# Feed-forward parts of a two-layer decoder trunk: product slabs spread over all tiles, two tiles per vector operation, whole weight rows split

## The chip, the cores and the metric

One NeuronCore of a Trainium2 chip runs the whole program in one launch. The metric is device time in microseconds (us); a lower number is better. Five engines matter here: TensorE (PE, with its weight loads shown apart as PEld), VectorE (DVE), ScalarE (ACT), GpSimd (POOL) and SyncE (SP), whose queue issues the DMAs.

## The reference

Two decoder layers over 256 tokens of width 2048, all in float32. What matters here is the feed-forward part that ends each layer (inner width 8192):

```python
def squared_relu_mlp(h, w1, w2):
    z = jax.nn.relu(h @ w1)
    return (z * z) @ w2

# in each layer i, after the mixer and the memory cross-attention
x = x + jnp.concatenate([token_out, mem_out], axis=-1) @ w_out[i]
x = x + squared_relu_mlp(rms_norm(x, ffn_norm[i]), w_ff1[i], w_ff2[i])
```

Around it stand a pooling mixer (layer 0), shared keys and values computed from the stream after layer 0, differential attention (layer 1) and a memory cross-attention in both layers.

## The kernel before

**Numbers in two parts.** Every float32 operand is split into a high part, rounded to the format that TensorE multiplies (`fp32r`), and a low part, the rest. A product then takes high x high, high x low and low x high. The activations are kept as `x[:, k, 0:256]` (high) and `x[:, k, 256:512]` (low) for each chunk k of 128 features. The weights are split while the kernel runs: `Feed._split` (L142) lets ScalarE copy a chunk of raw weights into `hi_ring` (L147, a cast) and VectorE subtract that from the raw chunk into `lo_ring` (L148).

**The feed.** All weights lie in device memory in the order of use, as rows of eight 128x128 blocks (128x1024, 512 KB). `Feed.load` (L116) issues one DMA for each on SyncE (L129), three ahead. A *job* is a piece of split weights. An ordinary job `("N", n)` is half a row, four blocks, and takes one slot of 512 columns in each ring; there are six slots. A slot is used again when the job in it has been multiplied. `Feed.fill` (L180) prepares up to three jobs ahead. A first run of the program without instructions (`dry`) records the order.

**A tile.** A narrow tile makes 128 output features for 256 tokens: 16 blocks, each with a matmul of 512 columns (high weights times both parts) and one of 256 columns (low weights times the high part). `a_part` (L361) alternates the two; `a_pairs` (L372) issues the two 512-column matmuls of a pair of blocks and then the two of 256. The framework assigns the instructions to fixed queues for each engine ahead of time, by readiness and priority; within one engine the order is then fixed.

**The feed-forward part**, `ffn(l, xs, tags, done)` (L636). There are 64 up tiles (`up_tile`) and, for output features 0 to 1023, four rounds q of eight down tiles (`down_tile`). Layer 0 uses the alternating order (L364 and L365 for up, L722 and L723 for down), layer 1 the paired one (L381, L383). Each up tile is copied out of PSUM by ScalarE (`evict`, L658), its two halves are added (L702), relu and scale follow (L284), ScalarE squares (L706), and high and low parts go to `z` (L662, L665). Each of these is issued for one tile. Output features 1024 to 2047 use a product scheme of the Strassen-Winograd kind with seven products where eight would be needed: a *slab* is the pair of activation chunks 2i and 2i+1 with a 2x2 arrangement of weight blocks 512 columns wide. It needs four sums of the activations (`combine`, `sums_high`, `sums_low`, kept in `sit`) and four of the weights. The weight sums are made by VectorE in the raw tiles: a step `K` (L166, L167) and one at L175. A slab has four jobs: 0 (two chunks), 1 (one), 2 (two), 3 (two); they give 6, 3, 6 and 6 matmuls of 512 columns (L748 to L750). Their results add up in seven PSUM banks (tiles `p`) over all 32 slabs of a layer.

**The order.** Sixteen up tiles run with three PSUM banks (`ff`). Then `open_banks` takes the seven product banks, and only one bank is left for tiles, `x_bank`. Rounds q = 0, 1, 2 run 24 tiles each, with a slab spread over every three: in the gap before the first tile job 0, before the second jobs 1 and 2, before the third job 3. The eight slabs of the last quarter and the last eight down tiles are left to `last` (L841): two slabs each ahead of tiles 0, 1 and 2, one each ahead of 3 and 4. `finish_banks` (L788) then combines the seven banks, and TensorE transposes the result (tile `ct`, L813). Work behind a tile is put off by `at(d, fn)`, which runs `fn` after d ticks; a narrow tile has four ticks.

Raw rows have four buffers and the raw tiles of slabs three, so that the second load of a slab waits until job 3 of the slab before has been split.

Of the kernel before, what the change touches and what calls it, by code (L numbers as in the profile page):

```python
# [18 lines left out]
P = 128  # L19
T = 256  # L20
# [5 lines left out]
NBLK = 5796  # L26
SLOTS, AHEAD, LOADS, KOFF, RAWS = 6, 3, 3, 2, 4
CN = 0.5 ** (1.0 / 3.0)
# [27 lines left out]
class Plan:  # L56
# [7 lines left out]
    def __init__(self):  # L64
        self.entries = []
        self.npos = 0
        self.jobs = []
        self.slabs = []

    def close(self):  # L70
# [9 lines left out]
        for p in prep:  # L80
            if p[0] == "K":
                self.loads += [("S", p[1], 0), ("S", p[1], 1)]
            elif p[0] == "N" and p[1] % 2 == 0:
                self.loads.append(("N", p[1] // 2))
            self.need[p] = len(self.loads) - 1
# [12 lines left out]
class Feed:  # L98


    def __init__(self, nc, wst, wpool, rows, plan, dry):
# [7 lines left out]
        self.t1 = None  # L109
        if not dry:  # L110
            self.hi = wpool.tile([P, SLOTS * 512], F32R, name="hi_ring")
            self.lo = wpool.tile([P, SLOTS * 512], F32R, name="lo_ring")
            self.busy = [False] * SLOTS
# [19 lines left out]
    def _slots(self, n):  # L133
        a = self.at if self.at + n <= SLOTS else 0
# [4 lines left out]
        self.at = (a + n) % SLOTS  # L139
        return a  # L140

    def _split(self, job, src, n):  # L142
# [3 lines left out]
        hi, lo = self.hi[:, a * 512 : (a + n) * 512], self.lo[:, a * 512 : (a + n) * 512]  # L146
# [5 lines left out]
    def _prepare(self, p):  # L152
        sub, add = self.nc.vector.tensor_sub, self.nc.vector.tensor_add
        self.load(self.plan.need[p] + 1 + LOADS)
        if p[0] == "N":
# [8 lines left out]
        t1 = self.t1[p[1] % 2]  # L164
        if p[0] == "K":
            add(t1, ra[:, 0:512], rb[:, 0:512])  # L166
            sub(rb[:, 0:512], t1, rb[:, 512:1024])  # L167
# [23 lines left out]

    def quad(self, what):

        job = ("N", self.pos // 4)
        if self.dry:
            self.plan.entries.append(what)
            if self.pos % 4 == 0:
                self.plan.jobs.append(job)
            return Nothing(), Nothing()
        if self.pos % 4 == 0:  # L200
# [9 lines left out]
    def used(self, n=1):  # L210
        self.pos += n
        if self.dry:
            self.plan.npos = self.pos
        elif self.pos % 4 == 0:
# [17 lines left out]
    def job_used(self, n, j):  # L232
        if not self.dry:
            self.free(("S", n, j))

# [11 lines left out]
def program(ctx, tc, plan, dry, xT, memT, par, lam, cst, wst, yT):  # L247
# [152 lines left out]
    def wide_step(ps, what, xs, k):  # L400
        hi, lo = feed.quad(what)
        for t in range(2):
            xh = xs[:, k, t * P : t * P + P]
            xl = xs[:, k, T + t * P : T + t * P + P]
            nc.tensor.matmul(ps[t], xl, hi, start=k == 0, stop=False)  # L405
            nc.tensor.matmul(ps[t], xh, hi, start=False, stop=False)  # L406
            nc.tensor.matmul(ps[t], xh, lo, start=False, stop=k == NK - 1)  # L407
# [3 lines left out]
    def b_tile(ps, w, l, c, xs):  # L411
        for k in range(NK):
            wide_step(ps, (w, l, k, c, 4), xs, k)
# [222 lines left out]
    def ffn(l, xs, tags, done):  # L636

        z = sp.tile([P, NK, 512], F32R, tag=tags[0], name=f"z{l}")
        sit = sp.tile([P, 8, 1024], F32R, tag=tags[1], name=f"sit{l}")
        room = sp.tile([P, 6144], F32, tag="big", name=f"room{l}")
        stage = [room[:, T * j : T * j + T] for j in range(8)]
        sums = [room[:, 2048 + 512 * j : 2560 + 512 * j] for j in range(2)]
        feed.t1 = [room[:, 3072 + 512 * j : 3584 + 512 * j] for j in range(2)]
        outs = [room[:, 4096 + 512 * j : 4608 + 512 * j] for j in range(3)]  # L650
        r = []
        banks = []
        cnt = [0]

        def evict(ps):
            x = outs[cnt[0] % 3]
            cnt[0] += 1
            nc.scalar.copy(x, ps)  # L658
            return x

        def high(j):
            nc.scalar.copy(z[:, j, 0:T], stage[j % 8])  # L662

        def low(j):
            nc.vector.tensor_sub(z[:, j, T : 2 * T], stage[j % 8], z[:, j, 0:T].bitcast(F32))  # L665

        def combine(i):

            a11, a21 = stage[2 * i % 8][:, 0:P], stage[2 * i % 8][:, P:T]
            a12, a22 = stage[(2 * i + 1) % 8][:, 0:P], stage[(2 * i + 1) % 8][:, P:T]  # L670
            s1, s2, s3, s4 = (sums[i % 2][:, c * P : c * P + P] for c in range(4))
            nc.vector.tensor_add(s1, a21, a22)
            nc.vector.tensor_sub(s3, a11, a21)
            nc.vector.tensor_sub(s2, s1, a11)
            nc.vector.tensor_sub(s4, a12, s2)

        def sums_high(i):
            nc.scalar.copy(sit[:, i, 0:512], sums[i % 2])

        def sums_low(i):  # L680
            nc.vector.tensor_sub(sit[:, i, 512:1024], sums[i % 2], sit[:, i, 0:512].bitcast(F32))

        def convert(j, d):
            at(d, lambda: high(j))
            at(d + 2, lambda: low(j))
            if j % 2:
                i = j // 2
                at(d + 3, lambda: combine(i))
                at(d + 5, lambda: sums_high(i))
                at(d + 7, lambda: sums_low(i))  # L690

        def up_tile(q, i, ps):
            if l == 1:
                a_pairs(ps, "w_ff1", l, q * NK + i, range(NK), xs)
            else:
                a_part(ps, "w_ff1", l, q * NK + i, range(NK), xs)
            if not r:
                r.append(rstd_from("x"))
            y = evict(ps)

            def first():
                nc.vector.tensor_add(y[:, 0:T], y[:, 0:T], y[:, T : 2 * T])  # L702
# [638 lines left out]
```

## Time and profile before

| | |
|---|---|
| runs (3) | median 2067.43 us, 2067.31 to 2068.43 |
| profiled execution, its span | 2069.3 us |
| TensorE busy | 2057.2 us, 99% |
| weight loads (overlap) | 1754.1 us, 85% |
| VectorE busy | 1727.0 us, 83% |
| ScalarE busy | 1352.3 us, 65% |
| moved by DMA | 390.77 MB, mean 189 GB/s |

The profile gives the profiled execution no other time than its span, from the first to the last instruction. In its rows, a start is counted from the start of the span; `L381` is a line of the kernel, `x_bank<-fx,hi_ring` the tile that is written and those that are read, with buffer numbers left out, and `[0.77 <-PE x_bank]` idle time before an instruction and what ended it. A matmul's length in the trace includes its way through the array, so consecutive ones overlap: start to start is what counts. A row such as `p<-hi_ring,sit` belongs to a slab's product.

### The profile page before, as it was taken

What the parts mean: (1) busy time and instruction counts of PE and PEld (TensorE: products, weight loads), DVE (VectorE), ACT (ScalarE), POOL (GpSimd) and SP (SyncE); (2) the same over time, 40 slices, a digit from 0 to 9 for tenths busy, and PEclk for the clock granted to TensorE, in tenths of its full rate; (3) what the DMA queues carried; (4) which work ended last, traced back from release to release, by engine and by line L of the source; (5) the groups of instructions that cost most, each with busy time, mean ns of one, the idle gap of its engine ahead of it and who ended that gap; (6) DMA issues with size and microseconds to landing.
All of it is one profiled execution on the core that took longest, in us unless ns stands there. A gap on an engine that the chain in (4) does not pass through costs nothing.

```text
span 2069.3 us, 32331 instructions
## 1 busy us (share of the span) xinstructions
PE 2057.2 (99%) x11086; PEld 1754.1 (85%) x11086; DVE 1727.0 (83%) x3231; ACT 1352.3 (65%) x2505; POOL 55.6 (3%) x67
## 2 busy tenths in 40 slices
PE   9999999999999999999999999999999999999998
PEld 7888888888888888878888888888888888888877
DVE  8788888889878878999766688888879978988897
ACT  7765566666666656668665687567666666766664
POOL 0001300000000000000000000310000000000000
PEclk9999999999999999999999999999999999999999
DMA  8555555555555555455565433555556555555554
GB/s 311 171 186 186 189 186 178 189 195 202 184 197 192 193 205 191 168 188 184 187 231 193 163 133 110 186 193 186 183 191 207 192 194 201 189 207 188 193 188 144
DMA packets 110471, 390.77 MB, mean 189 GB/s; under 512 B 12256, under 2 KB 14944, under 8 KB 110304
## 3 DMA queue, kind: packets, MB, share of 16 engines
q1 hardware_dynamic: 110160, 388.59, 55.7%
q8 instruction: 87, 1.43, 0.3%
q14 instruction: 80, 0.66, 0.1%
q10 hardware_dynamic: 144, 0.10, 0.0%
HBM read 386.54 MB, written 2.10 MB: 188 GB/s over the span
## 4 chain that ended last, share of the span: by engine, by line
PE 52%; ACT 1%; DVE 1%; DMA 0%; issue 0%; ACTq 0%; DVEq 0%
PE x_bank L381 14%; PE x_bank L383 7%; PE ff L381 3%; PE wo L364 3%; PE p L748 2%; PE p L750 2%; PE p L749 2%; PE ff L383 2%; PE wo L365 1%; PE k L405 1%; PE k L407 1%; PE v L405 1%; PE v L406 1%; PE k L406 1%; PE v L407 1%; PE q L405 1%
## 5 line engine op out<-in xcount | busy, mean ns | idle before, releaser
L147 ACT CAST hi_ring<-raw 128x512 fp32r<-128x512 f32 x1193 | 736.0, 621 | 525.9 <-PE x_bank L381 134.0
L148 DVE TENSOR_TENSOR lo_ring<-raw,hi_ring 128x512 fp32r<-128x512 f32 x1193 | 826.0, 700 | 222.6 <-ACT hi_ring L147 192.0
L148 DVE TENSOR_TENSOR lo_ring<-slab,hi_ring 128x1024 fp32r<-128x1024 f32 x192 | 234.5, 1222 | 47.3 <-ACT hi_ring L147 42.7
L364 PE MATMUL x_bank<-fx,hi_ring 128*128 128x512 f32 x768 | 271.7, 397 | 0.0
L147 ACT CAST hi_ring<-slab 128x1024 fp32r<-128x1024 f32 x192 | 200.8, 1047 | 69.1 <-PE p L749 27.2
L381 PE MATMUL x_bank<-fx,hi_ring 128*128 128x512 f32 x768 | 240.7, 395 | 0.0
L365 PE MATMUL x_bank<-fx,lo_ring 128*128 128x256 f32 x768 | 214.8, 280 | 0.0
L364 PE MATMUL wo<-cat,hi_ring 128*128 128x512 f32 x512 | 182.3, 401 | 0.0
L364 PEld LDWEIGHTS x_bank<-fx,hi_ring 128*128 128x128 f32 x768 | 144.1, 188 | 37.7 <-ACT room L658 0.5
L383 PEld LDWEIGHTS x_bank<-fx,lo_ring 128*128 128x128 f32 x768 | 144.3, 188 | 33.6
L722 PE MATMUL x_bank<-z,hi_ring 128*128 128x512 f32 x480 | 170.0, 396 | 1.4 <-ACT room L658 0.9
L381 PE MATMUL x_bank<-z,hi_ring 128*128 128x512 f32 x480 | 151.2, 395 | 0.4 <-ACT hi_ring L147 0.4
L383 PE MATMUL x_bank<-fx,lo_ring 128*128 128x256 f32 x768 | 150.9, 278 | 0.0
L365 PEld LDWEIGHTS x_bank<-fx,lo_ring 128*128 128x128 f32 x768 | 144.8, 189 | 0.7
L365 PE MATMUL wo<-cat,lo_ring 128*128 128x256 f32 x512 | 143.6, 281 | 0.0
L723 PE MATMUL x_bank<-z,lo_ring 128*128 128x256 f32 x480 | 134.3, 280 | 0.0
L381 PEld LDWEIGHTS x_bank<-fx,hi_ring 128*128 128x128 f32 x768 | 120.5, 189 | 3.7
L364 PEld LDWEIGHTS wo<-cat,hi_ring 128*128 128x128 f32 x512 | 96.1, 188 | 23.8 <-DVE cat L284 0.3
L722 PEld LDWEIGHTS x_bank<-z,hi_ring 128*128 128x128 f32 x480 | 90.1, 188 | 24.6 <-ACT room L658 1.5
L383 PEld LDWEIGHTS x_bank<-z,lo_ring 128*128 128x128 f32 x480 | 90.1, 188 | 21.8 <-DVE lo_ring L148 1.0
L748 PE MATMUL p<-hi_ring,sit 128*128 128x512 f32 x256 | 101.9, 398 | 1.7 <-ACT hi_ring L147 1.3
L749 PE MATMUL p<-hi_ring,sit 128*128 128x512 f32 x256 | 100.3, 392 | 0.0
(317 smaller groups left out, 4195.1 us busy)
## 6 DMA issues: line engine op xcount, KB each, us to landing
raw<-in_w SPq DMA_DIRECT2D x595, 512.0 KB, 3.5
slab<-in_w SPq DMA_DIRECT2D x128, 512.0 KB, 3.5
resid<-in_x SPq DMA_DIRECT2D x8, 256.0 KB, 5.5
memraw<-in_mem SPq DMA_DIRECT2D x4, 512.0 KB, 3.7
out_y<-resid SPq DMA_DIRECT2D x16, 128.0 KB, 1.9
memraw<-in_mem SPq DMA_DIRECT2D x7, 256.0 KB, 6.8
raw<-in_w SPq DMA_DIRECT2D x3, 256.0 KB, 3.3
memraw<-in_mem SPq DMA_DIRECT2D x2, 128.0 KB, 4.4
```

The lines of the kernel that those rows point to most:

```text
L147: self.nc.scalar.copy(hi, src)
L148: self.nc.vector.tensor_sub(lo, src, hi.bitcast(F32))
L364: nc.tensor.matmul(ps, hi, xs[:, k, :], start=first and i == 0, stop=False)
L365: nc.tensor.matmul(ps[:, T : 2 * T], lo, xs[:, k, 0:T], start=False, stop=last and i == len(ks) - 1)
L381: nc.tensor.matmul(ps, hi, xs[:, k % NK, :], start=k == ks[0], stop=False)
L383: nc.tensor.matmul(ps[:, T : 2 * T], lo, xs[:, k % NK, 0:T], start=False, stop=k == ks[-1])
L405: nc.tensor.matmul(ps[t], xl, hi, start=k == 0, stop=False)
L406: nc.tensor.matmul(ps[t], xh, hi, start=False, stop=False)
L722: nc.tensor.matmul(ps, hi, z[:, i, :], start=a, stop=False)
L723: nc.tensor.matmul(ps[:, T : 2 * T], lo, z[:, i, 0:T], start=False, stop=b)
L748: nc.tensor.matmul(ps, a[1], hi, start=first, stop=False)
L749: nc.tensor.matmul(ps, a[0], hi, start=False, stop=False)
```

## The change

The feed-forward part is rewritten. The matmuls stay the same in number and size.

- *Paired blocks*: `narrow` issues the paired order in both layers.
- *Slabs*: `slab_plan` gives every gap between tiles a list of slab jobs. A slab may run from the fourth tile on behind the second up tile of its pair (`LAG`). Slab 0 has its job 0 ahead of tile 5, so the banks open there. The usual spread over three gaps stays (jobs 0; 1 and 2; 3). Where slabs have fallen behind, or fewer than 12 tiles are left, a slab takes two gaps (0 and 1; 2 and 3); ahead of the first of the last eight tiles it takes one. Worked out for the 96 tiles: slabs 4, 5, 6 and 28, 30, 31 in two gaps, 29 in one, the other 25 in three; the last is done ahead of the fifth of the last eight tiles. Down tiles of a round no longer run as one group of eight: they stand between up tiles.
- *Rings of chunks*: `z` keeps 22 chunks and `sit` five slabs, in two tiles.
- *Two tiles per operation*: add, relu, square, high, low and the sums are issued once for a pair of up tiles, in `convert`.
- *Whole rows*: in the feed-forward parts a job `("R", n)` is a whole row, two slots, cast and subtracted in one instruction each. Two more ring slots (`extra`) make eight; a job of two chunks does not cross from slot 5 to 6.
- The weight sums reuse the raw tile (`t = rb[:, 0:512]`), one half of `K` moves behind job 1, four blocks are skipped ahead of layer 0's part to start at a whole row, and the first tile of the key projection takes its chunks in the order 8 to 15, 0 to 7.

```diff
+LAG = 4
 ...
     def close(self):
         prep = []
         for job in self.jobs:
+            if job[0] == "N" and job[1] // 2 in self.whole:
+                if job[1] % 2:
+                    continue
+                job = ("R", job[1] // 2)
             if job[0] == "S" and job[2] == 0:
                 prep.insert(max(0, len(prep) - KOFF), ("K", job[1]))
             prep.append(job)
 ...
     def _slots(self, n):
-        a = self.at if self.at + n <= SLOTS else 0
+        total = SLOTS + 2 if self.extra else SLOTS
+        a = self.at
+        if a < SLOTS < a + n:
+            a = SLOTS
+        if a + n > total:
+            a = 0
 ...
     def _prepare(self, p):
+        if p[0] == "R":
+            if not self._split(p, self.raw[("N", p[1])], 2):
+                return False
+            del self.raw[("N", p[1])]
+            return True
 ...
-        t1 = self.t1[p[1] % 2]
+        t = rb[:, 0:512]
         if p[0] == "K":
-            add(t1, ra[:, 0:512], rb[:, 0:512])
-            sub(rb[:, 0:512], t1, rb[:, 512:1024])
+            add(t, ra[:, 0:512], t)
             return True
-        src, n = ((ra, 2), (t1, 1), (rb, 2), (ra, 2))[p[2]]
+        src, n = ((ra, 2), (t, 1), (rb, 2), (ra, 2))[p[2]]
         if not self._split(p, src, n):
             return False
-        if p[2] == 0:
-            t2 = rb[:, 0:512].unsqueeze(1).to_broadcast([P, 2, 512])
+        if p[2] == 1:
+            sub(t, t, rb[:, 512:1024])
             two = ra.rearrange("p (a c) -> p a c", a=2)
-            sub(two, t2, two)
+            sub(two, t.unsqueeze(1).to_broadcast([P, 2, 512]), two)
 ...
+def slab_plan(tiles):
+    ready = {}
+    for t, what in enumerate(tiles):
+        if what[0] == "f" and what[1] % 2:
+            ready[what[1] // 2] = t + LAG
+    gaps = {}
+    t = ready[0]
+    for i in range(32):
+        t = max(t, ready[i])
+        groups = ((0,), (1, 2), (3,))
+        late = i - sum(ready[k] <= t for k in ready)
+        if late < -2 or t > len(tiles) - 12:
+            groups = ((0, 1), (2, 3))
+        if tiles[t] == ("d", 3, 0):
+            groups = ((0, 1, 2, 3),)
+        for g in groups:
+            gaps[t] = [(i, j) for j in g]
+            t += 1
+    return gaps
 ...
+        def convert(i, late):
+            y = both(i)
+            u, v = y[:, :, 0:T], y[:, :, T : 2 * T]
 ...
+            def add():
+                nc.vector.tensor_add(u, u, v)
+            def relu():
+                stt(u, u, 0.0, r[0].unsqueeze(1).to_broadcast([P, 2, T]), ALU.max, ALU.mult)
+            def square():
+                nc.scalar.activation(u, u, AF.Square)
 ...
+        def narrow(ps, w, n, ks, src):
+            for j in range(0, NK, 2):
+                two = []
+                for k in ks[j : j + 2]:
+                    two.append((k, *feed.block((w, l, k, n, 1))))
+                    feed.used()
+                for k, hi, lo in two:
+                    nc.tensor.matmul(ps, hi, src(k), start=k == ks[0], stop=False)
+                for k, hi, lo in two:
+                    nc.tensor.matmul(
+                        ps[:, T : 2 * T], lo, src(k)[:, 0:T], start=False, stop=k == ks[-1]
+                    )
 ...
+        tiles = [("f", j) for j in range(NK)]
         for q in range(3):
+            n = 0
+            for j in range(NK):
+                tiles.append(("f", NK * q + NK + j))
+                for _ in range((0, 2, 2, 1, 1, 1, 1)[j] if j < 7 else 0):
+                    tiles.append(("d", q, n))
+                    n += 1
+        ups = len(tiles)
+        tiles += [("d", 3, n) for n in range(8)]
+        gaps = slab_plan(tiles)
+        runs = {}
+        def go(part):
+            for t in part:
+                for i, j in gaps.get(t, ()):
+                    if not banks:
+                        open_banks()
+                    if i not in runs:
+                        runs[i] = slab_jobs(i)
+                    runs[i](j)
+                    if (i, j) == (31, 3):
+                        finish_banks()
+                        banks.append(None)
+                if t >= len(tiles) - 3:
+                    feed.extra = None
+                ps = mmt("ff") if len(banks) != 7 else bank()
+                if tiles[t][0] == "f":
+                    up_tile(tiles[t][1], ps)
+                else:
+                    down_tile(*tiles[t][1:], ps)
 ...
+    feed.skip(("w_ff1", 0, 0, 0, 4))
     x_in = []
     down = ffn(0, fx, ("S1", "S0"), lambda n: resid_done(n, [(x_in[0], G_KV)], False))
 ...
+    late = list(range(8, NK)) + list(range(8))
-        b_tile(ps, "w_kv", 0, c, x_kv)
+        b_tile(ps, "w_kv", 0, c, x_kv, late if c == 0 else range(NK))
```

More of the change, by code (lines that the diff above doesn't have):

```diff
@@ L213, in used @@
             self.plan.npos = self.pos
+        elif (self.pos - 1) // 8 in self.plan.whole:
+            if self.pos % 8 == 0:
+                self.free(("R", self.pos // 8 - 1))
         elif self.pos % 4 == 0:
@@ L636, in ffn @@
     def ffn(l, xs, tags, done):
[L644 to L650, printed above, removed]
+        ZS, SS = 22, 5
@@ L651, in ffn @@
+        za = sp.tile([P, NK, 512], F32R, tag=tags[0], name=f"za{l}")
+        zb = sp.tile([P, NK, 512], F32R, tag=tags[1], name=f"zb{l}")
+        room = sp.tile([P, 4096], F32, tag="big", name=f"room{l}")
+        feed.extra = None if dry else sp.tile([P, 2048], F32R, tag="half", name=f"slot{l}")
+        feed.rows_whole = True
+        pairs = [room[:, 1024 * j : 1024 * j + 1024] for j in range(3)]
+        douts = [room[:, 3072 + 512 * j : 3584 + 512 * j] for j in range(2)]
         r = []
@@ L652, in ffn @@
         banks = []
[L653 to L675, printed above, removed]
```

244 lines of the change are left out of this document (131 added, 113 removed).

## The prediction

> **What bounds the kernel now.** I read the page first, then the busy times by stage, then the timeline of TensorE with ScalarE.
>
> ```profile
> span 2069.3 us, 32331 instructions
> ...
> PE 2057.2 (99%) x11086; PEld 1754.1 (85%) x11086; DVE 1727.0 (83%) x3231; ACT 1352.3 (65%) x2505; POOL 55.6 (3%) x67
> ```
>
> and, from its list of DMA issues (KB each, us to landing),
>
> ```profile
> slab<-in_w SPq DMA_DIRECT2D x128, 512.0 KB, 3.5
> ```
>
> TensorE is busy 99% of the span, so only three things can shorten the run: fewer matmuls, matmuls that follow each other faster, or the waits that are left. The change issues the same matmuls. I therefore cut both feed-forward parts at the first matmul of each stage (the sixteen tiles without slabs, the 24 slabs spread over 72 tiles, the last eight tiles with eight slabs, layer 0 and then layer 1, and the end of the run). Columns: length, then PE, PEld, DVE, ACT and POOL busy, the granted clock (1.00, full), DMA share and GB/s.
>
> ```profile
> 256.30:347.20 90.90, 90.90 (x516) 78.87 (x515) 73.11 (x149) 62.97 (x119) 1.79 (x2) 1.00 0.53 176
> 347.20:867.60 520.40, 520.40 (x2811) 444.15 (x2810) 445.38 (x770) 339.40 (x575) 0.00 (x0) 1.00 0.57 194
> 867.60:959.60 92.00, 88.97 (x443) 71.07 (x442) 89.52 (x138) 64.45 (x108) 0.00 (x0) 1.00 0.52 177
> 1368.70:1458.30 89.60, 89.60 (x516) 78.18 (x515) 72.99 (x149) 62.81 (x119) 1.79 (x2) 1.00 0.54 179
> 1458.30:1973.90 515.60, 515.60 (x2811) 444.79 (x2811) 443.93 (x768) 339.51 (x575) 0.00 (x0) 1.00 0.57 196
> 1973.90:2058.30 84.40, 81.32 (x397) 64.93 (x396) 78.18 (x111) 50.59 (x74) 0.00 (x0) 1.00 0.51 169
> 2058.30:2069.30 11.00, 7.33 (x63) 7.12 (x61) 3.93 (x7) 0.47 (x1) 0.00 (x0) 1.00 0.37 121
> ```
>
> The first two stages have TensorE busy throughout; in the last one TensorE loses time while VectorE is busy 89.5 of 92.0 us and 78.2 of 84.4. There VectorE, not TensorE, sets the pace.
>
> ```profile
> 1701.59 0.40 PE L748 MATMUL p<-hi_ring,sit 128*128 128x512 f32 x1
> ...
> 1703.63 0.39 PE L381 MATMUL x_bank<-z,hi_ring 128*128 128x512 f32 x1
> ...
> 1709.20 0.40 PE L748 MATMUL p<-hi_ring,sit 128*128 128x512 f32 x1
> ```
>
> ```profile
> 2058.09 0.27 PE L813 MATMUL ct<-const,c_a 128*128 128x128 f32 x1
> 2058.20 0.27 PE L813 MATMUL ct<-const,c_b 128*128 128x128 f32 x1
> ```
>
> These starts give the undisturbed prices of layer 1: a paired tile 1709.20 - 1703.63 = 5.57 us, a gap of nine product matmuls 2.04. A slab with its three tiles takes 515.6 / 24 = 21.48, so a slab alone 21.48 - 3 x 5.57 = 4.77.
>
> **The change part by part.** *Paired blocks* (layer 0 alone; layer 1 has them already). Same matmuls, other order: the stage of sixteen tiles goes from 90.9 to 89.6 us (-1.3) and the 24 slabs from 520.4 to 515.6 (-4.8), if layer 0 then runs as layer 1 does. Gain 6.1.
>
> A rule speaks against this term. The Trainium skill's page "TensorE: Matmul & The Clock Gate", section "Wait — 56ns, not 53.3ns?", gives start-to-start as N / 2.4 GHz plus about 2.5 ns, whatever the order; by it pairing would bring 0 and the forecast would be 6.1 us later. The trace does not agree: two stages with equal matmul counts, differing in that order, are 1.3 us apart.
>
> *Slabs that trail the tiles.* Now the eighth part of the slabs, eight per layer, falls on the last eight tiles. By `slab_plan`, slab 0 starts before tile 5, the list runs in three gaps per slab (6, 9, 6 matmuls), and only slabs 4 to 6 and 28 to 31 are packed tighter (two gaps, slab 29 in one); the last three tiles carry none. What the last stage would take at undisturbed prices: layer 0, 8 x 5.57 + 8 x 4.77 + 16 transposes of about 0.1 = 84.3 against 92.0, so 7.7 is lost; layer 1 up to its last tile, 7 x 5.57 + 8 x 4.77 + 0.4 = 77.6 against 84.4, so 6.8. Together 14.5 over 16 crowded slabs, 0.9 each. In the new list about two slabs per layer (29 and a neighbour) stand as crowded: 4 x 0.9 = 3.6; I keep 4 us, with 0 and 14.5 as bounds. Ceiling 6.1 + 14.5 = 20.6, after this rest 16.6.
>
> *Two tiles per vector operation, whole rows split.*
>
> ```profile
> L147 ACT CAST hi_ring<-raw 128x512 fp32r<-128x512 f32 x1193 | 736.0, 621 | 525.9 <-PE x_bank L381 134.0 <-PE x_bank L364 83.0 <-PE wo L364 67.5
> L148 DVE TENSOR_TENSOR lo_ring<-raw,hi_ring 128x512 fp32r<-128x512 f32 x1193 | 826.0, 700 | 222.6 <-ACT hi_ring L147 192.0 <-PE p L749 13.9 <-PE tr L523 5.2
> L148 DVE TENSOR_TENSOR lo_ring<-slab,hi_ring 128x1024 fp32r<-128x1024 f32 x192 | 234.5, 1222 | 47.3 <-ACT hi_ring L147 42.7 <-PE x_bank L364 4.5
> L147 ACT CAST hi_ring<-slab 128x1024 fp32r<-128x1024 f32 x192 | 200.8, 1047 | 69.1 <-PE p L749 27.2 <-PE x_bank L381 14.8 <-PE x_bank L722 12.6
> ...
> L702 DVE TENSOR_TENSOR room<-room 128x256 f32<-128x256 f32 x128 | 53.5, 418 | 0.2 <-ACT room L658 0.2
> ...
> L681 DVE TENSOR_TENSOR sit<-room,sit 128x512 fp32r<-128x512 f32 x64 | 44.0, 687 | 0.7 <-ACT sit L678 0.7
> ```
>
> A row costs one 1.05 cast and one 1.22 subtraction for two of 0.62 and 0.70: 0.19 and 0.18 us less, over 384 rows 75 us of ScalarE and 68 of VectorE. Three operations of 0.42 on each of two tiles (the add of L702, the relu and the low part, all 128x256) become three of 0.69 on both (as L681's 128x512), 0.45 less per pair, 64 pairs, 29 us. All of it lies beside TensorE, so by itself it is worth nothing; it is the cover for the crowded slabs.
>
> The cost is in one place. While the seven product banks are open a tile has one PSUM bank (`x_bank`), so its eviction by ScalarE must end inside the gap of product matmuls that follows. A six-matmul gap, from the tile's last two matmuls to the next tile's first:
>
> ```profile
> 1580.09 0.39 PE L383 MATMUL x_bank<-fx,lo_ring 128*128 128x256 f32 x2
> ...
> 1580.29 0.62 ACT L147 CAST hi_ring<-raw 128x512 fp32r<-128x512 f32 x1 [0.77 <-PE x_bank L381]
> ...
> 1580.82 0.58 ACT L658 COPY room<-x_bank 128x512 f32<-128x512 f32 x1
> ...
> 1581.69 0.39 PE L381 MATMUL x_bank<-fx,hi_ring 128*128 128x512 f32 x1
> ```
>
> The tile's last weights free ring slots, a cast takes ScalarE at once, and the eviction queued behind it ends at 1581.40, 0.29 before the next tile. With a cast of 1024 columns the same two instructions looked so, in the crowded stage where nobody waited:
>
> ```profile
> 2006.74 1.05 ACT L147 CAST hi_ring<-slab 128x1024 fp32r<-128x1024 f32 x1 [0.24 <-DVE slab L167]
> ...
> 2007.70 0.57 ACT L658 COPY room<-x_bank 128x512 f32<-128x512 f32 x1
> ```
>
> From cast start to eviction end 1.53 us. Put into the gap above: 1580.29 + 1.53 = 1581.82, and where a tile did wait for the eviction,
>
> ```profile
> 940.48 0.58 ACT L658 COPY room<-x_bank 128x512 f32<-128x512 f32 x1
> ...
> 941.12 0.50 PE L722 MATMUL x_bank<-z,hi_ring 128*128 128x512 f32 x1 [0.89 <-ACT room L658]
> ```
>
> it started 0.06 after it and its first matmul took 0.11 longer (0.50 for 0.39). So 1581.88 for 1581.69: 0.19 lost, with the longer matmul 0.30. Which cast is freed there follows from the ring: eight slots hold four two-slot jobs, so the end of a tile frees the job four places on. Before job 0 that is job 1 of the slab (one chunk, 0.62, no loss); before job 3 it is job 0 of the next slab, two chunks; before jobs 1 and 2 it is a row, but that gap is 2.04 long. 25 slabs per layer keep three gaps, so 50 gaps of this kind: 50 x 0.19 = 9.5, upper bound 50 x 0.30 = 15, lower bound 0 (the eviction is queued first). Below zero is out, since no gap gets shorter. I take 10, nearest to the row in which the wait itself is seen.
>
> *Edits with no cost.* The four skipped blocks pad one load. The second load of a slab waits for job 3 of the slab before and lands in 3.5 us; its first reader, job 1, comes over a tile and a gap (6.9 us) after that job's matmuls; without this cover up to 3.5 per slab. Banks opened at tile 5, the key projection beginning with chunk 8 and the shared key buffer wait for work that ended earlier. SyncE issues as many loads, in an order moved by one row.
>
> *Sum.* 6.1 + 14.5 - 4 - 10 = 6.6 us off a span of 2069.3. The runs have a median of 2067.43, 1.9 below that span; I take the same 6.6 off it: 2060.8.
>
> **The rivals.** (1) *The eviction goes first*, or finds ScalarE free. For it: ScalarE has less to do; against: in the gap above the cast started at once. Then 20.6 - 4 = 16.6: 2050.8.
> (2) *The end stays crowded*: slabs 28 to 31 lie within seven tiles, and VectorE remains the pace there. Then the 14.5 stay, 6.1 - 10 = -3.9, 2071.3 at the most; at half of them 2064.
> (3) *Slower: the row after jobs 1 and 2 comes late.* That row's slots come free 4.8 us before its use (a row of 2.78 and the gap of 2.04). Its split takes 1.05 + 1.22; with a whole slab's own work ahead on VectorE (a 1.22 subtraction, a 0.69 and another 1.22) it is 5.4, so 0.6 late in each of 64 slabs, 38 us less the 16.6: 2089. It decides from 16.6 / 64 = 0.26 us per slab. Against it:
>
> ```profile
> DVE lo_ring L148 <- ACT hi_ring L147: 234.7, 388, 2.5
> ```
>
> VectorE itself waits 388 times for the cast, so it has no backlog in the even stages (445 of 520 us busy, less after the change).
> (4) *Pairing brings nothing* because layer 0 was slower for another reason than the order of its blocks: 6.6 - 6.1 = 0.5, 2066.9. The Trainium skill's page named above leads here; the two stages of sixteen tiles speak against it.
>
> **How the numbers follow.** Forecast 0.45, (1) 0.27, (2) 0.08, (3) 0.16, (4) 0.04. About 0.2% (4.1 us) is what can be told from no change: faster means under 2063.3. The forecast's own range is 2055 to 2067 (bounds 0.30 and 0.07 per gap): four fifths of it, all of (1) and a little of the rest give 0.66 faster; its last fifth, (4) and half of (2) 0.17 the same; (3) and what is left of (2) 0.17 slower. The range reaches from below (1) with 2 us of crowding, 2048, to the end of (2), 2071; most of (3) stays outside.
>
> **What would show it.** Layer 0's tiles at 5.57 us; last stages near 84 and 78 us with VectorE below TensorE; casts of 128x1024 from the raw tiles, 384 at 1.05. For the forecast against (1): waits of TensorE for the eviction copy, some 50 of 0.2 to 0.3 us, all in front of a tile that follows job 3 of a slab. For (3): TensorE waiting for `lo_ring` behind jobs 1 and 2. I am wrong altogether if the even stages no longer run at 21.48 per slab for a reason outside these waits.

## The result, and the profile after

| | median, us | range | runs |
|---|---|---|---|
| before | 2067.37 | 2066.54 to 2068.43 | 4 |
| after | 2057.32 | 2056.45 to 2059.45 | 4 |

The ratio is 0.995 (95% interval 0.9936 to 0.9964): 10.05 us faster, between 7.4 and 13.2. The forecast was 2060.8 in a range from 2048 to 2071. The page of the profile after:

```profile
span 2056.1 us, 30582 instructions
...
PE 2049.2 (100%) x11086; PEld 1751.9 (85%) x11086; DVE 1666.0 (81%) x2591; ACT 1273.0 (62%) x1993; POOL 56.5 (3%) x67
...
slab<-in_w SPq DMA_DIRECT2D x128, 512.0 KB, 4.0
```

The matmuls are the same 11086. VectorE and ScalarE lost 61 and 79 us of work (before: 1727.0 and 1352.3), and the span is 13.2 us shorter. To see where, both kernels are cut at the first matmul of each feed-forward part and at its end. Busy times by stretch, in the columns of the prediction (length, PE, PEld, DVE, ACT, POOL, clock, DMA share, GB/s); first the kernel before, layer 0 and layer 1:

```profile
256.35:959.56 703.21, 700.18 (x3765) 594.01 (x3764) 607.91 (x1055) 466.78 (x802) 1.79 (x2) 1.00 0.56 190
1368.75:2065.35 696.60, 693.52 (x3780) 594.89 (x3778) 598.55 (x1032) 453.39 (x768) 1.79 (x2) 1.00 0.56 190
```

and the kernel after, the two parts and then two stretches of layer 0, the even stage and the one with slabs 28 to 31:

```profile
256.30:948.97 692.67, 692.64 (x3764) 593.06 (x3763) 577.91 (x738) 425.13 (x541) 1.50 (x2) 1.00 0.56 192
1358.46:2052.18 693.72, 693.12 (x3779) 593.89 (x3778) 569.38 (x714) 414.20 (x514) 2.22 (x2) 1.00 0.56 191
...
418.70:872.20 453.50, 453.50 (x2460) 387.75 (x2459) 372.22 (x464) 270.79 (x335) 0.00 (x0) 1.00 0.56 194
872.20:924.85 52.65, 52.62 (x278) 44.62 (x276) 48.31 (x64) 37.45 (x50) 0.00 (x0) 1.00 0.50 173
```

Layer 0 gained 10.5 us and layer 1 2.9; what lies between the parts is as long as before. The gain differs because only layer 0 got the paired blocks. One profile is one execution: in a second one of the kernel before (e10) layer 1's part took 695.34, and against that layer 1 gained 1.6. In the last stretch TensorE is now busy 52.62 of 52.65 us with VectorE below it: the crowding is gone. The even stage runs at 453.50 / 21 = 21.60 us a slab, 0.12 more than the 21.48 of before, and the gaps in which job 3 runs show why (the timeline of layer 1, TensorE, its weight loads and ScalarE):

```profile
1401.09 0.39 PE L792 MATMUL x_bank<-fx,lo_ring 128*128 128x256 f32 x2
...
1401.29 1.05 ACT L165 CAST hi_ring<-slab 128x1024 fp32r<-128x1024 f32 x1 [0.73 <-PE x_bank L790]
...
1402.24 0.58 ACT L802 COPY room<-x_bank 128x512 f32<-128x512 f32 x1
...
1402.69 0.39 PE L862 MATMUL p<-hi_ring,za 128*128 128x512 f32 x1
...
1402.87 0.30 PEld L790 LDWEIGHTS x_bank<-fx,slot 128*128 128x128 f32 x2 [0.22 <-ACT room L802]
1402.91 0.70 PE L790 MATMUL x_bank<-fx,slot 128*128 128x512 f32 x2
```

The tile ends, the cast of the next slab's job 0 takes ScalarE for 1.05 us, the eviction (L802: the copy of the tile's bank out of PSUM) stands behind it until 1402.82, and the next tile's weight load waits for it. This is the forecast's mechanism. One thing is new: the matmul at 1402.69 is a seventh product. TensorE's order is fixed ahead of time, and one matmul of the next slab's job 0 was drawn into the wait; the gap after the tile has five instead of six. The waits of the weight loads in layer 0's part (us in total, times, longest):

```profile
PEld x_bank L790 <- ACT room L802: 3.6, 15, 0.3
PEld x_bank L790 <- ACT room L824: 2.4, 11, 0.2
```

26 waits, and 26 in layer 1 too. In each layer 25 of them stand in front of a tile that follows job 3 of a slab, behind a cast of 128x1024 for job 0, with a seventh product in the gap; the other one (0.18 us) follows slab 29.

### The profile page after: what moved, and what is told of

It is laid out like the page before. It is cut to its first block, busy times and chain, and to the rows that moved or that the text cites. A ratio compares the mean times of both kernels' runs of the same rounds, so it can differ in the third digit from the quotient of the medians.

```text
span 2056.1 us, 30582 instructions
## 1 busy us (share of the span) xinstructions
PE 2049.2 (100%) x11086; PEld 1751.9 (85%) x11086; DVE 1666.0 (81%) x2591; ACT 1273.0 (62%) x1993; POOL 56.5 (3%) x67
## 4 chain that ended last, share of the span: by engine, by line
PE 97%; ACT 1%; DVE 1%; DMA 1%; issue 0%; SPq 0%; DVEq 0%; ACTq 0%
PE x_bank L790 31%; PE x_bank L792 15%; PE wo L431 6%; PE p L862 5%; PE p L863 5%; PE p L864 5%; PE ff L790 3%; PE wo L432 3%; PE u L431 2%; PE ff L792 2%; PE u L432 1%; PE k L473 1%; PE k L474 1%; PE k L475 1%; PE q L473 1%; PE q L475 1%
## 5 line engine op out<-in xcount | busy, mean ns | idle before, releaser
L165 ACT CAST hi_ring<-raw 128x512 fp32r<-128x512 f32 (+1 forms) x725 | 576.3, 799 | 407.9 <-PE x_bank L790 187.5
L166 DVE TENSOR_TENSOR lo_ring<-raw,hi_ring 128x512 fp32r<-128x512 f32 (+1 forms) x725 | 668.3, 928 | 181.8 <-ACT hi_ring L165 162.8
L790 PEld LDWEIGHTS x_bank<-fx,hi_ring 128*128 128x128 f32 x1376 | 215.2, 189 | 10.2 <-ACT room L802 3.7
L166 DVE TENSOR_TENSOR lo_ring<-slab,hi_ring 128x1024 fp32r<-128x1024 f32 (+1 forms) x182 | 187.4, 1033 | 20.2 <-ACT hi_ring L165 19.9
L165 ACT CAST hi_ring<-slab 128x1024 fp32r<-128x1024 f32 (+1 forms) x182 | 163.0, 898 | 49.2 <-PE x_bank L790 44.3
L790 PE MATMUL x_bank<-za,hi_ring 128*128 128x512 f32 x592 | 186.1, 396 | 0.0
L790 PE MATMUL x_bank<-fx,slot 128*128 128x512 f32 x512 | 162.3, 398 | 0.0
L792 PEld LDWEIGHTS x_bank<-za,lo_ring 128*128 128x128 f32 x592 | 111.2, 188 | 26.0
L166 DVE TENSOR_TENSOR slot<-raw,slot 128x1024 fp32r<-128x1024 f32 x84 | 103.1, 1227 | 32.8 <-ACT slot L165 32.8
L792 PE MATMUL x_bank<-za,lo_ring 128*128 128x256 f32 x592 | 116.3, 278 | 0.0
L792 PE MATMUL x_bank<-fx,slot 128*128 128x256 f32 x512 | 100.6, 278 | 0.0
```

The costliest lines, as they stand in the source:

```text
L165: self.nc.scalar.copy(hi, src)
L166: self.nc.vector.tensor_sub(lo, src, hi.bitcast(F32))
L790: nc.tensor.matmul(ps, hi, src(k), start=k == ks[0], stop=False)
L792: nc.tensor.matmul(ps[:, T : 2 * T], lo, src(k)[:, 0:T], start=False, stop=k == ks[-1])
```

## Experiments

Each experiment ran on one chip together with new runs of the kernel before, whose medians were 2068.2 to 2069.6; so ratios are compared, and inside a profile the lengths of the two parts.

### The order of blocks: e1, e11, e10

**e1**, the kernel before with pairs in layer 0 as well:

```diff
-            if l == 1:
-                a_pairs(ps, "w_ff1", l, q * NK + i, range(NK), xs)
-            else:
-                a_part(ps, "w_ff1", l, q * NK + i, range(NK), xs)
+            a_pairs(ps, "w_ff1", l, q * NK + i, range(NK), xs)
...
-            if l == 1 and not end:
+            if not end:
```

> The kernel before, with one part of the change: layer 0's narrow tiles also run their blocks in pairs (hi, hi, lo, lo). Theory (pairing is worth its row difference, 15.71 to 15.77 us a plain stage step against the unpaired one): 6.1 us less than the kernel before, 2061.3, all of it in layer 0's feed-forward part, whose tiles go from about 5.68 to 5.57 us. Rival (a matmul's start-to-start time does not depend on the order of blocks, as the Trainium skill's clock-gate page has it): no change, 2067.4 within 1 us.

Measured 2062.32 us, ratio 0.9966 (0.9952 to 0.9979), 4.3 to 9.9 us less. Layer 0's part of e1:

```profile
254.82:950.72 695.90, 694.09 (x3765) 593.42 (x3763) 606.58 (x1052) 466.51 (x802) 1.80 (x2) 1.00 0.57 192
```

7.3 us shorter than before, on the forecast's 6.1; VectorE's work is unchanged. Of the 7.3, 6.0 lie in the two stages that the forecast counted (89.60 and 515.67 us for 90.88 and 520.36) and 1.3 in the last one (90.63 for 91.97). The rival falls.

**e11** turns it round: the kernel after, with blocks alternating in both layers.

```diff
-                for k, hi, lo in two:
-                    nc.tensor.matmul(ps, hi, src(k), ...)
-                for k, hi, lo in two:
-                    nc.tensor.matmul(ps[:, T : 2 * T], lo, src(k)[:, 0:T], ...)
+                for k in ks[j : j + 2]:
+                    hi, lo = feed.block((w, l, k, n, 1))
+                    nc.tensor.matmul(ps, hi, src(k), ...)
+                    nc.tensor.matmul(ps[:, T : 2 * T], lo, src(k)[:, 0:T], ...)
```

> The kernel after with the narrow tiles' blocks alternating again (hi, lo, hi, lo) in both layers; everything else as after. Theory (the order sets the pitch; layer 0 lost about 6 to 7 us by it): tiles of 5.63 to 5.69 us where the slab's gap does not hide it, 6 to 7 us more in each layer, 2069 to 2072. Rival (the pitch is a matter of the execution): tiles of 5.56 in at least one of the layers, 2057 to 2064, or runs that differ by 6 us and more among themselves.

Measured 2073.59 us, ratio 1.0019 (1.0010 to 1.0028) where after had 0.995. The two parts:

```profile
256.91:958.14 701.23, 701.23 (x3765) 595.79 (x3763) 579.04 (x738) 425.58 (x541) 1.50 (x2) 1.00 0.59 190
1368.05:2070.32 702.27, 702.11 (x3779) 596.77 (x3778) 571.29 (x715) 414.68 (x514) 2.22 (x2) 1.00 0.58 189
```

8.6 us more in each layer, with TensorE busy throughout. Most tiles between products take 5.64 us where after had 5.56, and the weight loads of layer 0 wait only 1.5 us more for evictions than in after: most of the cost is in the matmuls, not in waits. The profiled execution was one of the longest; by the ratios the difference is some 14 us, 7 a layer. The rival, tiles of 5.56 in one of the layers, falls.

**e10**, the kernel before once more, because a stage with alternating blocks outside the feed-forward parts had two lengths in kernels whose code there is the same.

> The kernel before, unchanged, for a second profile. Alternating blocks (hi, lo, hi, lo) ran in the projection by `wo` of layer 0 at 176.9 ns a matmul in the profiles of before, after, e2 and e3 and at 174.2 in those of e1, e4, e5, e6, e8 and e9, whose code there is the same. Theory (the slower pitch of alternating blocks is fixed by their order): layer 0's feed-forward part takes 703.2 us again, its sixteen free tiles 90.9, as in the first profile. Rival (the pitch differs from execution to execution, so a second execution may have it at the faster pitch in layer 0 as well): the part takes 696 to 698, the sixteen tiles 89.6, without any edit.

Measured 2069.25 us, ratio 1.0 (0.999 to 1.001). The first row is layer 0's sixteen free tiles in the first profile, the next two are the same tiles and the rest of the part in the second profile:

```profile
256.35:347.23 90.88, 90.88 (x516) 78.85 (x515) 73.09 (x149) 62.97 (x119) 1.79 (x2) 1.00 0.53 176
```

```profile
256.34:345.63 89.29, 89.29 (x517) 78.05 (x515) 73.05 (x149) 62.98 (x119) 1.79 (x2) 1.00 0.55 180
345.63:959.24 613.61, 610.20 (x3250) 516.00 (x3249) 534.73 (x907) 403.69 (x683) 0.00 (x0) 1.00 0.57 192
```

A split verdict. The sixteen tiles ran 1.6 us faster with no edit, as the rival said; the whole part, 702.90, came out as the theory said, but only because the rest was 1.3 us longer than in the first profile (613.61 for 612.33). Between products, tiles of alternating blocks took 5.64 or 5.55 us, both in one profile; paired ones took 5.56, in a few places 5.59, wherever they waited for nothing. At its fast pace the alternating order is no slower than the paired one: sixteen tiles took 89.29 here and 89.60 in pairs.

### The eviction behind the cast: e2 and e6

**e2**, the kernel after with job 0's cast in halves:

```diff
-        self.nc.scalar.copy(hi, src)
+        if job[0] == "S" and job[2] == 0:
+            for c in (0, 512):
+                self.nc.scalar.copy(hi[:, c : c + 512], src[:, c : c + 512])
+        else:
+            self.nc.scalar.copy(hi, src)
```

> The kernel after, with the cast of each slab's job 0 (128x1024 on ScalarE) cut into two of 512 columns, so that the eviction copy can go in between the halves. Theory (the eviction held behind the two-chunk cast delays the tile behind each six-matmul gap): the waits of the weight load for the evicted bank, 15 of 0.3 us and 11 of 0.2 us a layer, go, and the tiles behind job 3 fall from 5.64-5.68 to 5.56 us: 50 gaps of 0.10 us, 5 us less, about 2052.3. Rival 1 (the long gap comes from the switch between job and tile and not from ScalarE's queue): no change, 2057.3 within 1 us. Rival 2 (each more instruction on ScalarE costs its fixed part, and the second half still stands in front of the eviction): 0 to 3 us slower.

Measured 2052.20 us, ratio 0.9917 (0.9904 to 0.9931). The gap that was shown of after, and the two parts:

```profile
1398.85 0.62 ACT L167 CAST hi_ring<-slab 128x512 fp32r<-128x512 f32 x1
...
1399.72 0.62 ACT L167 CAST hi_ring<-slab 128x512 fp32r<-128x512 f32 x1 [0.25 <-PE x_bank L794]
...
1400.25 0.58 ACT L806 COPY room<-x_bank 128x512 f32<-128x512 f32 x1
...
1401.12 0.39 PE L794 MATMUL x_bank<-fx,slot 128*128 128x512 f32 x1
```

```profile
256.95:946.97 690.02, 689.99 (x3765) 594.93 (x3764) 580.45 (x738) 431.80 (x573) 1.50 (x2) 1.00 0.60 193
1356.89:2047.95 691.06, 690.33 (x3780) 595.71 (x3778) 572.22 (x715) 420.74 (x546) 2.22 (x2) 1.00 0.59 192
```

The eviction does not go in between the halves, as the expectation had it: in all 50 gaps both halves stand in front of it. But in 49 of them the first half now starts while the tile is still being multiplied (here at 1398.85), so that only 0.62 us are in front of the eviction after the tile's end, where the whole cast had 1.05. The eviction ends 0.29 before the next tile; gaps have six products again, all whole tiles between the products but two take 5.56 to 5.57 us, and each part is 2.65 us shorter. That is the price of the 50 waits behind job 3: 5.3 us, 0.11 each.

**e6**, the kernel after with six slots:

```diff
-        feed.extra = None if dry else sp.tile([P, 2048], F32R, tag="half", name=f"slot{l}")
+        feed.extra = None
```

> The kernel after, without the two extra ring slots of the feed-forward parts: six slots, so three two-slot jobs. A row's slots come free only one row (2.78 us) before its first matmul, and its cast and subtraction take 1.05 + 1.22 = 2.27. Theory (the third rival's mechanism, late rows, is real and the two slots are the cover that kept it away): a few tenths of a us at many rows behind a slab's job, 20 to 60 us slower than the kernel after, 2077 to 2117, with TensorE waiting for lo_ring. Rival (ScalarE and VectorE are idle a fifth of the time and start each split at once): 2.27 fits into 2.78, within 5 us, 2057 to 2062.

Measured 2084.27 us, ratio 1.0075 (1.0059 to 1.0090): some 26 us slower than after by the ratios, in the theory's range, but not by its mechanism. Waits of the weight loads in layer 0's part, and one gap:

```profile
PEld x_bank L790 <- ACT room L802: 13.8, 31, 0.5
PEld x_bank L790 <- ACT room L824: 8.1, 18, 0.5
PEld x_bank L792 <- DVE lo_ring L166: 1.1, 3, 0.4
```

```profile
435.60 0.39 PE L792 MATMUL x_bank<-za,lo_ring 128*128 128x256 f32 x2
...
435.80 1.05 ACT L165 CAST hi_ring<-raw 128x1024 fp32r<-128x1024 f32 x1 [1.73 <-PE x_bank L790]
...
436.76 0.58 ACT L824 COPY room<-x_bank 128x512 f32<-128x512 f32 x1
...
437.39 0.50 PE L790 MATMUL x_bank<-fx,hi_ring 128*128 128x512 f32 x1
```

Late splits (`lo_ring`) are three short waits. With three two-slot jobs in the ring instead of four, the end of a tile frees the job three places on, and that is a two-chunk cast in front of nearly every six-matmul gap: 49 waits for the eviction, and here no seventh product fills them. The part took 706.33 us, 16.3 more than in e2: 0.33 a wait, or 0.31 without the 1.1 us of late splits.

### The crowded last stages: e3, e4, e5, e8, e9

**e3**, the kernel before without the weight sums of the last eight slabs of each layer:

```diff
+        if p[0] == "K" and p[1] % 32 >= 24:
+            return True
...
-        if p[2] == 0:
+        if p[2] == 0 and p[1] % 32 < 24:
```

> The kernel before, with the weight sums of the last eight slabs of each layer left out (the additions and subtractions on VectorE that make a slab's combined chunks; their splits and matmuls stay, on unsummed weights): a part of the computation is left out. Theory (the last stages of before are paced by VectorE, 0.9 us a crowded slab): the last stages, 92.0 us in layer 0 and 84.4 us in layer 1, fall to within 2 us of 84.3 and 77.6, so 10 to 14.5 us less, about 2055. Rival (they are paced by something else that comes with the crowding, such as the free slots of the split rings or the order of the jobs): less than 3 us, 2064 to 2067.

Measured 2058.33 us, ratio 0.9947 (0.9935 to 0.9960), 8.3 to 13.4 less. One tile with two slabs in front of it, in the kernel before and then in e3:

```profile
1990.37:2006.81 16.44, 16.12 (x76) 12.48 (x75) 16.08 (x21) 9.26 (x13) 0.00 (x0) 1.00 0.60 194
```

```profile
1982.44:1997.56 15.12, 15.12 (x76) 12.72 (x75) 11.65 (x15) 9.91 (x13) 0.00 (x0) 1.00 0.67 220
```

VectorE was busy 16.08 of 16.44 us; without the sums it has 11.65 to do, and TensorE runs the tile and the two slabs in 15.12, 5.57 + 2 x 4.77 = 15.11 at the prediction's prices. VectorE was the pace there. The parts are 6.7 and 5.7 us shorter, but 1.6 of the 6.7 lie in the sixteen tiles without slabs, which e3 does not touch and which ran at their fast pace (89.30 us). The last stages by themselves, to the end of each part, in before and then in e3:

```profile
867.59:959.56 91.97, 88.94 (x443) 71.04 (x442) 89.49 (x138) 64.41 (x108) 0.00 (x0) 1.00 0.52 178
1973.89:2065.35 91.46, 88.38 (x458) 71.99 (x456) 81.69 (x117) 51.06 (x74) 0.00 (x0) 1.00 0.50 166
```

```profile
865.85:953.00 87.15, 86.26 (x442) 71.69 (x441) 74.16 (x118) 64.11 (x108) 0.00 (x0) 1.00 0.57 187
1967.34:2052.93 85.59, 84.91 (x458) 72.83 (x456) 65.79 (x94) 50.89 (x74) 0.00 (x0) 1.00 0.54 177
```

They lost 4.8 and 5.9 us, 10.7 together, or 10.1 against the second profile of before (92.84 and 89.96). In layer 0 the expected 84.3 was missed by 2.9, more than the 2 us that were allowed. What e3 leaves are other waits of the weight loads in these stages: in layer 0 1.2 us for an eviction and 1.9 for late splits, in layer 1 1.3 for late splits. The kernel after has none of them.

**e4**, the kernel after with the small operations back:

```diff
+        if job[0] == "R":
+            for c in (0, 512):
+                h, s = hi[:, c : c + 512], src[:, c : c + 512]
+                self.nc.scalar.copy(h, s)
+                self.nc.vector.tensor_sub(lo[:, c : c + 512], s, h.bitcast(F32))
+        else:
...
-                nc.vector.tensor_add(u, u, v)
+                for c in range(2):
+                    nc.vector.tensor_add(u[:, c, :], u[:, c, :], v[:, c, :])
```

and so for relu, square, high and low.

> The kernel after, with the small operations back: whole rows split in two halves of 512 columns on ScalarE and VectorE, and the add, relu, square, high and low steps run per tile instead of per pair of tiles. The even spread of slab jobs, the larger ring and the pairing stay. Theory (the even spread of the slabs takes the crowding away; the wider vector operations only lower VectorE's share): within 2 us of the kernel after, 2056 to 2060, with VectorE's busy share up from 81% to some 85%. Rival (the wider operations are what takes VectorE off the path): the last stages lose 8 to 14 us again, 2065 to 2071.

Measured 2059.33 us, ratio 0.9953 (0.9941 to 0.9966); after had 0.995. The parts:

```profile
256.04:949.15 693.11, 693.08 (x3764) 593.16 (x3763) 600.79 (x1025) 463.96 (x794) 1.79 (x2) 1.00 0.59 192
1358.74:2053.62 694.88, 693.11 (x3779) 593.94 (x3778) 590.33 (x999) 453.22 (x766) 1.79 (x2) 1.00 0.59 191
```

0.4 and 1.2 us longer than after, with 23 and 21 us more work on VectorE. The spread does it without the wide operations. These are worth at most 1.6 us in the profiles, and the ratios do not tell the two kernels apart.

**e5, e8, e9** ask whether the wide operations would also have done it alone. All three crowd slabs 24 to 31:

```diff
-        t = max(t, ready[i])
+        t = max(t, ready[i], 60 + i if i >= 24 else 0)
...
-        late = i - sum(ready[k] <= t for k in ready)
-        if late < -2 or t > len(tiles) - 12:
-            groups = ((0, 1), (2, 3))
-        if tiles[t] == ("d", 3, 0):
+        if i >= 24:
             groups = ((0, 1, 2, 3),)
```

e8 has the small operations of e4 besides, e9 those but whole rows.

> The kernel after, with the last eight slabs of each layer crowded again: slabs 24 to 31 wait and run whole (21 product matmuls in one gap), one in front of each tile, the last four tiles free of them. The wide vector operations, the pairing and the eight slots stay. Theory (only the spread took the crowding away; VectorE needs, for a crowded slab with its tile, 0.69 + 1.22 + 0.69 + 0.69 + 3 x 1.22 for the slab, 2 x 1.22 for the rows, some 1.7 for residual and norm, 11.1 us against 10.33 of TensorE, even with wide operations): 0.7 lost on each of sixteen slabs, 11 us, 2066 to 2070. Rival (the wide operations, 0.36 less per tile on VectorE and the eviction off its queue, would have cured the crowding by themselves): within 3 us of the kernel after, 2057 to 2060.

> The kernel of e5 (slabs 24 to 31 crowded, one whole slab in front of each tile) with the small operations of e4: rows split in two halves, and the add, relu, square, high and low steps per tile. In the crowded stretch of e5 VectorE is busy 75.47 of 76.65 us and TensorE loses nothing. Theory (what was lost in the last stages of before was VectorE's work above TensorE's, and either the spread or the wide operations take it away): 16 rows more at 0.18 and four to eight pairs at 0.45 make 80 to 82 us of VectorE in 76.65, so 4 to 5 us a layer more than e5, 2085 to 2088. Rival (something else of the kernel before, such as its last three tiles with slabs, lost the time): within 2 us of e5, 2076 to 2080.

> The kernel of e8 with whole rows split again (one cast and one subtraction of 1024 columns), the steps per tile stay small. Theory: only the pairs' 0.45 remain above e5, four to eight a stretch, 77 to 79 us of VectorE in 76.65: 0.5 to 2 us a layer more than e5, 2079 to 2082; the rows give most of the difference to e8. Rival (two tiles per operation is what counts): near e8.

Measured 2078.21 (ratio 1.0046, 1.0033 to 1.0058), 2071.30 (1.0012, 1.0002 to 1.0021) and 2077.24 us (1.0038, 1.0023 to 1.0052). All three expectations missed: e8 should have been the slowest and is the fastest. Layer 0, the seven tiles left without slabs and then the crowded stretch, in e5 and in e8:

```profile
795.26:844.32 49.06, 40.73 (x224) 34.54 (x225) 28.79 (x39) 22.99 (x30) 0.00 (x0) 1.00 0.50 160
850.85:927.52 76.67, 76.67 (x391) 64.59 (x390) 75.49 (x95) 52.42 (x68) 0.00 (x0) 1.00 0.57 186
```

```profile
795.06:841.43 46.37, 40.61 (x226) 34.41 (x224) 30.39 (x58) 25.41 (x48) 0.00 (x0) 1.00 0.53 168
848.25:924.60 76.35, 76.27 (x389) 64.58 (x388) 75.95 (x115) 54.91 (x88) 0.00 (x0) 1.00 0.58 188
```

One slab a tile costs TensorE nothing in either: VectorE just keeps up; how much of that it owes to the slack of the seven tiles in front was not separated. The expectation had added up the lengths of VectorE's instructions, 11.1 us for a slab and a tile against 10.33 of TensorE. In the stretch of 76.67 us, 7.4 times 10.33, the lengths do add up to 83.6 us, 11.3 each, but neighbours overlap in the trace and VectorE is busy for 75.49, 10.2 each. Before had crowded two slabs before a tile, 16.08 us of VectorE for 15.11. The time went into the seven tiles that the edit left without products between them: with one bank, each waits for the whole eviction, and 7 x 5.56 = 38.9 us became 49.06, 10 us in each layer. Where whole rows are cast (e5, e9) that wait holds a 1.05 us cast in front of the eviction, in e8 one of 0.62: 2.7 us less over seven tiles, 0.38 each. It is the eviction behind a cast once more, at another place. Whether wide operations alone would carry two slabs a tile was not tried.

### The best version: e7

**e7** is e2 with the blocks in pairs in `a_part` too.

> The kernel after with the half casts of job 0, and with the blocks of the two projections that still alternate (the queries' `u` and the mixers' `wo`, in a_part) taken in pairs as in the feed-forward parts. In the profile of after four alternating blocks take 1.409 to 1.421 us and four paired ones 1.393 to 1.394; 704 blocks are 176 groups of four, 0.016 to 0.028 each. Theory (the pitch is set by the order of the blocks everywhere): 3 to 5 us less than with the half casts alone, 2047 to 2049.5. Rival (the gain of pairing belongs to the feed-forward parts, where the ring is busier): no change, 2052 within 1 us.

Measured 2051.04 us, ratio 0.9915 (0.9901 to 0.9928): faster than before and after, but not to be told from e2 (0.9917). The row that the expectation rested on is of the wandering kind. The `wo` projection of layer 0, same code, in after and in e8:

```profile
162.31:256.30 93.99, 93.99 (x542) 81.65 (x540) 77.83 (x122) 49.73 (x86) 26.12 (x29) 1.00 0.53 186
```

```profile
162.06:254.67 92.61, 92.61 (x542) 81.50 (x540) 75.95 (x123) 49.29 (x89) 25.70 (x29) 1.00 0.59 189
```

and in e7, in pairs, between the two:

```profile
161.65:254.66 93.01, 92.79 (x542) 80.99 (x540) 74.74 (x122) 49.51 (x86) 24.90 (x29) 1.00 0.60 187
```

The medians of e2 and e7 differ by 1.2 us, less than the runs of one kernel do; a gain here is not shown.

## Why the prediction was right, term by term

| term | forecast | the runs |
|---|---|---|
| paired blocks in layer 0 | -6.1 | -7.3 (e1) |
| crowding of before | -14.5 | -13.1 (6.3 in e1, 6.8 in before; the weight sums alone 10.7 in e3) |
| crowding that stays | +4 | +0.8 |
| eviction behind the cast | +10 | +5.3 (e2) |
| a late slab load, once | none | +1.0 |
| sum | -6.6 | -13.3 |

The 6.3 are e1's last stage of 90.63 us less the 84.3 at the prediction's undisturbed prices.

The first profiles differ by 13.4 us in the two parts (10.5 + 2.9), so the list is complete within 0.1, closer than two profiles of one kernel agree. Taken from the second profile of before, the terms add up to 11.5 and the parts differ by 11.9. The spans differ by 13.2 and 11.6, the timed medians by 10.05: the first profile of before, from which the forecast took all its prices, was a long execution (2069.3, the second 2067.7).

The mechanisms held, but two costs were put 8 us too high together. By the terms the runs gained twice what was forecast (13.3 us for 6.6); that the timed change of 10.05 lies nearer to 6.6 is luck. The range from 2048 to 2071 also held rivals 1 and 2, so the time alone decides little: the 50 waits do.

**Pairing.** The size held and rival 4 fell (e1, e11), but one of its two rows was worth less than it seemed: the 1.3 us of the sixteen tiles lies within what one kernel does by itself (90.88 and 89.29). The row of the 24 slabs was the sound one.

**Crowding.** VectorE as the pace was right (e3), and that the spread removes it (e4). The 7.7 us of layer 0 were worked out at 5.57 us a tile, the price of paired blocks, so up to 8 x 0.08 = 0.6 us of them belong to the order of blocks. The average of 0.9 a slab was made of three tiles with two slabs each and two tiles with one, and e5 and e8 show that one a tile loses nothing by itself. So the rest of 4 us, two crowded slabs a layer at the average, was too much: behind slab 29 two tiles and twelve products take 14.23 us for 13.85, so TensorE loses some 0.4 us a layer. Rival 2 fell. The forecast gave the wide operations no worth of their own, and e4 agrees. Its 97 us less for VectorE are lengths of instructions; since neighbours overlap, the busy time fell by 61.

**The eviction.** This step was mis-sized. Its place, its count (50) and its cause are confirmed by e2, and rival 1, that the eviction goes first, fell. The price of 0.19, from a row of before in which nothing was moved, was 0.11 (above the lower bound of 0.07, which the prediction does not derive): the seventh product filled 0.23 of the wait. Where no product was drawn in, in e6, a wait cost 0.31 to 0.33, a little above the upper bound of 0.30. The forecast kept the gap at six matmuls although the order of TensorE's queue is made anew for each program; that is the step which failed.

**The late rows** of rival 3 did not appear with eight slots. e6 shows what the two slots that the forecast did not cost are worth, some 26 us, and that even then the loss comes by ScalarE's order and not by late splits.

**Edits taken at nothing.** The second load of a slab was one of them, with "up to 3.5" if its cover is gone. The prediction has job 1 as its first reader. It is the weight sum of step `K` (L189), which stands ahead of job 0. In after the load was felt once, in layer 1. VectorE waited for the slab's data in front of the weight sum, and everything queued behind that (the relu, then ScalarE's square, then a cast) came late (waits and timeline of after, 1430 to 1450 us):

```profile
DVE slab L189 <- DMA slab<-in_w: 2.3, 1, 2.3
PEld p L862 <- ACT hi_ring L165: 1.0, 1, 1.0
```

```profile
1439.26 0.69 DVE L189 TENSOR_TENSOR slab<-slab,slab 128x512 f32<-128x512 f32 x1 [2.27 <-DMA slab<-in_w]
...
1443.52 0.63 ACT L751 ACTIVATE room<-room 128x512 f32<-128x512 f32 x1 [3.23 <-DVE room L351]
```

Over the whole run VectorE waited 42 times in this place,

```profile
DVE slab L189 <- DMA slab<-in_w: 42.0, 42, 2.7
```

but only this one reached TensorE, whose weight loads waited for job 0's cast in no other place. The same gap of layer 1 is longer than its neighbours in e2, e4, e5, e7, e8 and e9 too, by 0.2 us (e5, e9) to 2.0 (e8).

## What to carry to other kernels

Where a bank or buffer is single, look at which instruction the freeing of the previous one releases on the evicting engine: one long instruction in front of the eviction is paid on every turn, and cutting that instruction in two, so that its first half need not wait for the end of the tile, added 13 us to ScalarE's 1273 us of work and bought 5 us here. When an average loss over a stage is moved to a new layout, first split it by how dense each piece was. A difference between two stretches of one profile is a sound price only if a second profile of the same kernel keeps it.

## What was not expected of the hardware

Matmuls with alternating weights and widths (512 columns on the high block, 256 on the low) have two paces: `wo` 93.99 or 92.61 us, sixteen tiles 90.88 or 89.29, from one execution or program to the next, at a granted clock of 1.00 throughout. Paired, a tile that waited for nothing took 5.56 to 5.57 us in nearly every place (5.59 in a few). The Trainium skill's page "TensorE: Matmul & The Clock Gate", section "Wait — 56ns, not 53.3ns?", has one start-to-start time for the full clock, N / 2.4 GHz plus about 2.5 ns; an estimate by it is 16 x (215.8 + 109.2) ns = 5.20 us a tile, less than any tile here, and it has no second pace at that clock. The measurement decides. What sets the pace stays open: no run here looked for it below the order of the blocks.
